# Two layer norms finished in place during the following stage, value tiles cleared one projection later

## The chip, the cores and the metric

The kernel runs on one core of a Trainium2 chip. The metric is the device time of one execution in microseconds (us); the time before is the median of three executions. Names of engines: PE (TensorE, matrix products and transposes), DVE (VectorE), ACT (ScalarE), POOL (GpSimd), SP (SyncE, here only an issuer of DMAs). ACT issues DMAs too, on a queue of its own, in order with its computations.

## The reference

Two transformer blocks over 256 tokens of width 1024, in float32. The change lies in the first of them:

```
def _layer_norm(x, g, b):
    mu = jnp.mean(xf, axis=-1, keepdims=True)
    var = jnp.mean(jnp.square(xf - mu), axis=-1, keepdims=True)
    return ((xf - mu) * lax.rsqrt(var + LN_EPS)).astype(x.dtype) * g + b

for i in range(DEPTH):                       # DEPTH = 2
    h = swa(x) if i % 2 == 0 else nsa(x)     # window attention / sparse attention
    x = _layer_norm(DN_ALPHA * x + h, ln_gain[i, 0], ln_bias[i, 0])
    f = swiglu(x) if i % 2 == 0 else moe(x)  # 3584 hidden / 8 experts, 2 a token
    x = _layer_norm(DN_ALPHA * x + f, ln_gain[i, 1], ln_bias[i, 1])
```

So there are four layer norms, counted 0 to 3. Number 0 stands between the window attention and the SwiGLU, number 1 between the SwiGLU and the sparse attention. Each result is used twice: as the input of the next matrix products, and, untransposed, as the x of the next residual sum. The second block (a mixer, a cross-attention to 256 memory tokens, a feed-forward layer) follows; its memory tokens depend on nothing before them.

## The kernel before

The 256 tokens are two tiles of 128 rows, tt = 0 and 1 (in the orders and rows a tile name such as X or y stands for both, unless a number tells them apart). The stages are built one after the other: `swa`, `ffn0`, `nsa`, `moe`, then the second block. A float32 product is three matmuls: high part by high part, high by low, low by high. Weights come from HBM through SP's queue into nine raw tiles of 512 KB (`w`); ACT copies out the high half (`wh`, lines 253 and 256), DVE subtracts to get the low half (`wl`, lines 254 and 257), into a ring of five split tiles from which PE reads. A 512 KB tile of `ffn0` feeds 24 matmuls.

The instructions of each engine run in one fixed order that a scheduler works out when the kernel is built, from dependences, priorities and memory: a tile that finds no free on-chip memory waits in that order until a pool is closed. `issue_after(i)` adds that what follows may not be placed ahead of instruction i; it adds no wait on the chip.

A layer norm 0 or 1 goes as follows. `ln_part` makes the residual sum y and its statistics (lines 374, 375). `ln_norm` normalises y in place (line 397, two halves of 512 columns), PE transposes it (line 186), and `transpose_split` puts gain and bias on the transposed tile (lines 201 on DVE, 203 on ACT, tile `trg`) and splits it into `xh` (line 204, ACT) and `xl` (line 205, DVE), the input of the next products. `ln_end` then makes the untransposed result: gain and bias rows are broadcast to all partitions by two DMAs of 512 KB on ACT's queue (`gb`, `bb`), and X = y * gb + bb takes eight DVE operations of 128x512 (lines 441, 442).

Inside `ffn0`, after the second chunk of hidden columns, `memory_tokens` loads the memory tokens (tile `mem`, one buffer, twice 512 KB, line 1867), squares and scales them (lines 1872 to 1875) and has PE transpose them for a later product. At the start of `nsa`, small tables (`cm`, `vhalf`, `cval`, `pr`, `w2`) are loaded on ACT's queue, and the value tiles `vz` (lines 845, 846) and `kcc` are cleared behind the emission of the first projection (columns 1024 to 1535, which ends in the rotated tiles `two`, lines 823, 824). In the attention proper, with the pool `nsa3` open, PE fills waits with products of the memory tokens (line 1900).

`route_load` brings the router's weights `rt` and three tables (`first`, `slots`, `uf`) by DMA on ACT's queue and puts the gain of layer norm 2 on the weights (`gb` again, line 968; column sums, line 970). `moe` then makes the logits: PE multiplies by `gb` (line 1002), DVE adds the norm's parts (lines 1007, 1008, tile `L`), picks two experts a token (lines 1014 to 1022, `sel`, `selb`), PE counts places (lines 1025 to 1029), and a branch on the counts follows. Four tiles of 1 MB (`parked`) of the experts' weights are loaded at that time.

Of the kernel before, what the change touches and what calls it, by code (L numbers as in the profile page):

```python
# [8 lines left out]
F32 = mybir.dt.float32  # L9
# [3 lines left out]
OP = mybir.AluOpType  # L13
AX = mybir.AxisListType
PSUM = bass.MemoryType.PSUM

P = 128
D = 1024
# [6 lines left out]
def f(ap):  # L25
    return ap.bitcast(F32)
# [72 lines left out]
class Net:  # L99
# [287 lines left out]
    def ln_norm(self, tt):  # L387

        nc = self.nc
        idx = self.ln  # L390
        if idx == 2:
            return self.ln_rows(tt)
        mu, rs = self.ln_stats(tt)
        y = self.y[tt]
        for h in range(2):
            yh = y[:, h * 512:h * 512 + 512]
            nc.vector.tensor_scalar(yh, yh, mu, rs, op0=OP.subtract, op1=OP.mult)
        if not self.ln_xT:
            self.new_xT()
            self.ln_xT = True  # L400
        gc = self.cols[:, idx * 8:(idx + 1) * 8]
        bc = self.cols[:, 32 + idx * 8:32 + (idx + 1) * 8]
        self.transpose_split(y, KD, self.xh[:, :, tt * P:(tt + 1) * P], self.xl[:, :, tt * P:(tt + 1) * P], gc, bc)
# [23 lines left out]
            nc.scalar.copy(Xh[:, s], y[:, s])  # L427
            nc.vector.tensor_sub(self.Xl[:, tt, s], y[:, s], f(Xh[:, s]))

    def ln_end(self):  # L430

        nc, A = self.nc, self.A
        li, lj = divmod(self.ln, 2)
        with self.pool("lng", 1) as lp:
            gb = self.bcast(A["ln_gain"][li, lj], D, "gb", pool=lp)
            bb = self.bcast(A["ln_bias"][li, lj], D, "bb", pool=lp)
            for tt in range(2):
                x = self.xp.tile([P, D], F32, tag=f"X{tt}", name=f"X{tt}")
                for c in range(0, D, 512):
                    cs, e = slice(c, c + 512), (nc.vector, nc.vector)[tt]  # L440
                    e.tensor_mul(x[:, cs], self.y[tt][:, cs], gb[:, cs])
                    e.tensor_add(x[:, cs], x[:, cs], bb[:, cs])
                self.X[tt] = x


    def rope64(self, pool, src, tt, nh, pairs=False):
# [55 lines left out]
    def heads_out(self, oh, ol, W, idx):  # L502

        def view(w, r0, nk, c0, n):
            for half in range(2):
                r = r0 // 512 * 512 + r0 % 512 // 2 + half * 256
                src = W[r:r + nk * 64, c0:c0 + n]
                self.nc.sync.dma_start(w[half * 64:half * 64 + 64, :, :n], src.rearrange("(g d) n -> d g n", d=64))

        self.ln_begin(idx)  # L510
        self.gemm(lambda k, tt: (oh[:, k, tt * P:(tt + 1) * P], ol[:, k, tt * P:(tt + 1) * P]), W, KD,
                  [(0, 512), (512, 512)], self.ln_part, view=view, apart=(1,))
        self.fine = False
        if idx == 0:
            self.ln_end()

    def swa(self):
        nc, A, tc = self.nc, self.A, self.tc
# [95 lines left out]
    def ffn_body(self, Wg, g0, Wu, u0, dff, Wd, emit, scale=None, beside=lambda p: None):  # L614

        nc, tc = self.nc, self.tc
        nkf = dff // P
        chunks = [(j, min(512, dff - j)) for j in range(0, dff, 512)]
        with ExitStack() as c:
            p = c.enter_context(self.pool("ffn", 1))  # L620
# [11 lines left out]
            j, n = chunks[0]  # L632
# [20 lines left out]
            for j, n in chunks[1:]:  # L653
                s = p.tile([P, 4, T], F32, tag="silT", name="sil", bufs=2)
                k0 = j // P

                def gate(b, ps):
                    x = s[:, 2 * b:2 * b + 2]
                    if R is not None:
                        nc.vector.tensor_mul(x, ps, R.unsqueeze(1).to_broadcast([P, 2, T]))  # L660
                    nc.scalar.activation(x, x if R is not None else ps, AF.Silu)

                def up(b, ps):
                    x, k = s[:, 2 * b:2 * b + 2], k0 + 2 * b
                    nc.vector.tensor_mul(x, x, ps)
                    nc.scalar.copy(hh[:, k:k + 2], x)
                    nc.vector.tensor_sub(hl[:, k:k + 2], x, f(hh[:, k:k + 2]))

                self.gemm_f(Wg, g0 + j, n, gate)
                self.gemm_f(Wu, u0 + j, n, up)  # L670
                if j == 512:
                    beside(p)
# [22 lines left out]
    def ffn0(self):  # L695
        A = self.A
        self.ln_begin(1)
        self.mems = ExitStack()
        p = self.mems.enter_context(self.pool("memt", 1))
        self.mhl = [p.tile([P, 8, T], F32R, name=f"mem{n}") for n in "hl"]  # L700
        self.ffn_body(A["ffn_w_gate"][0], 0, A["ffn_w_up"][0], 0, 3584, A["ffn_w_down"][0], self.ln_part, beside=self.memory_tokens)
        self.ln_end()


    def nsa(self):
        nc, A, tc = self.nc, self.A, self.tc
        self.fine = True
        with ExitStack() as c0:
            po = c0.enter_context(self.pool("heads", 1))
            po.tile([P, 16], F32, name="lead")  # L710
            c = c0.enter_context(ExitStack())
            p = c.enter_context(self.pool("nsa", 1))
# [3 lines left out]
            zero = p.tile([P, 1], F32, name="zero")  # L716
            nc.vector.memset(zero, 0.0)
            vz = {b: [p.tile([P, 2, 4, P], F32R, name=f"v{b}{n}") for n in "hl"] for b in "sw"}
# [3 lines left out]
            kcc = [p.tile([P, 2, 2, 16], F32R, name=f"kc{n}") for n in "hl"]  # L722
            gate = [p.tile([P, 16, 3], F32, name=f"gate{tt}") for tt in range(2)]
            cm = p.tile([P, 2, 16], F32, name="cm")
            nc.scalar.dma_start(cm, A["cmask"].rearrange("t p c -> p t c"))
            cmb = p.tile([P, 2, 16], BF16, name="cmb")
            nc.vector.tensor_copy(cmb, cm)
            vhalf = p.tile([96, P], F32, name="vhalf")
            nc.scalar.dma_start(vhalf, A["vhalf"])
            cval = p.tile([P, 2], F32, name="cval")  # L730
            nc.scalar.dma_start(cval, A["cvalid"].rearrange("t p c -> p (t c)"))
            with ExitStack() as cc:
                self.turns = 1
                cp = cc.enter_context(self.pool("cmp", 1))
# [1 line left out]
                pos = cp.tile([P, 2, 16], F32, name="pos")  # L736
                for i, n in enumerate(("b_cmp_pos_k", "b_cmp_pos_v")):
                    pr = cp.tile([16, P], F32, tag="pr", name="pr")
                    nc.scalar.dma_start(pr, A[n][0].rearrange("(j l) d -> j (l d)", l=2))
                    tp = self.tr.tile([P, 512], F32, tag="tr", name="tr")  # L740
                    nc.tensor.transpose(tp[:, :16], pr, self.idn[:16, :16])
                    nc.vector.tensor_copy(pos[:, i], tp[:, :16])
                w2 = cp.tile([P, 2, 2, 2, 64], F32, name="w2")
                for i, n in enumerate(("b_cmp_k_w2", "b_cmp_v_w2")):
                    for h in range(2):
                        nc.scalar.dma_start(w2[:, i, :, h], A[n][0].rearrange("(k p) d -> p k d", p=P))


                def windows(which, two):
# [63 lines left out]
                def emit(i, c0, n, ps, tts=(0, 1)):  # L813
                    if c0 == 1024:
                        twos = self.twos = self.twos if tts[0] else [[], []]
                        two = self.two = self.two if tts[0] else po.tile([P, 2, 2, 4, 2, 64], F32, tag="oh", name="two")
                        for tt in tts:
                            u, t = self.rope64(a2, ps[tt][:, :256].rearrange("p (h d) -> p h d", d=64), tt, 4)
                            for w in range(2):
                                twos[w].append(two[:, w, tt])  # L820
                            v = ps[tt][:, 256:512].rearrange("p (h d) -> p h d", d=64)
                            both = lambda x: x.unsqueeze(2).to_broadcast([P, 4, 2, 64])
                            nc.vector.tensor_add(twos[0][tt], both(u), both(t))
                            nc.scalar.copy(twos[1][tt], both(v))
                    for tt in tts:
                        if c0 == 1536:
                            self.k_heads(a2, ps[tt][:, :256], kT["s"], tt)
# [12 lines left out]

                W = A["b_w_in"][0]
                self.gemm(self.xs, W, KD, [(1024, 512)], emit, apart=(0,))
                for z in vz["s"] + vz["w"]:
                    z = z.rearrange("p s v d -> p (s v d)")
                    nc.vector.tensor_copy(z[:, :512], zero.to_broadcast([P, 512]))
                    nc.scalar.copy(z[:, 512:], zero.to_broadcast([P, 512]))
                for k in kcc:
                    nc.gpsimd.tensor_copy(k.rearrange("p c h j -> p (c h j)"), zero.to_broadcast([P, 64]))
                self.gemm(self.xs, W, KD, [(1536, 512)], emit)
                win = windows(0, self.twos[0])  # L850
                self.gemm(self.xs, W, KD, [(2048, 256)], emit)
# [38 lines left out]
            for cc in range(2):  # L890
                for tt in range(2):
# [4 lines left out]
                    for half in range(2):  # L896
# [6 lines left out]
                        for b in range(4 // nh):  # L903
# [6 lines left out]
                                                     start=i == 0 and n == 0, stop=False)  # L910
                            nc.tensor.matmul(own, self.idb, self.maskb[:, 1:2].to_broadcast([P, 2 * nh, P]), start=False, stop=True)
                            gs = slice(b * nh, b * nh + nh)
                            nc.vector.tensor_reduce(nm[:, gs], sc.rearrange("p i r s j -> p i r (s j)"), axis=AX.X, op=OP.max, negate=True)
                            for i in range(nh):
                                g = b * nh + i
                                for r in range(2):
# [7 lines left out]
                        for r, br in enumerate("sw"):  # L924
                            for st in range(nst):
# [9 lines left out]
                                nc.tensor.matmul(ops, vl, ph, start=False, stop=False)  # L935
                                nc.tensor.matmul(ops, vh, pl, start=False, stop=False)
                        self.fill(1 / 16, SOON)
                    tp = self.tr.tile([96, 4, P], F32, tag="tr", name="tr")
                    for g in range(4):
                        nc.tensor.transpose(tp[:, g], f(pc[tt][:, cc * 4 + g]).rearrange("p n j -> p (n j)"), self.idn)  # L940
# [919 lines left out]
    def memory_tokens(self, p):  # L1860

        nc, A = self.nc, self.A
        h, l = self.mhl
        gc = self.cols[:, self.col["mem_kv_norm_2"]:self.col["mem_kv_norm_2"] + 8]
        for tt in range(2):
# [283 lines left out]
```

## Time and profile before

| | |
|---|---|
| median of 3 executions | 2332.0 us (2325.09 to 2341.94) |
| the profiled execution | 2328.03 us, span of the trace 2326.2 us |
| PE busy | 2229.0 us, 96% of the span |
| DVE busy | 1799.7 us, 77% |
| ACT busy | 1477.1 us, 63% |
| mean granted TensorE clock | 0.980 of full speed |

The stages by the trace, in us from the start of the span: window attention to about 100, SwiGLU to 342, projections of the sparse attention to about 436, attention and output product to 578, routing to 596, experts to about 1570, second block to the end. "Granted clock" is the share of the full TensorE clock that the chip allowed in a stretch; it is 1.0 or 0.5.

### The profile page before, as it was taken

What the parts mean: (1) busy time and instruction counts of PE and PEld (TensorE: products, weight loads), DVE (VectorE), ACT (ScalarE), POOL (GpSimd) and SP (SyncE); (2) the same over time, 40 slices, a digit from 0 to 9 for tenths busy, and PEclk for the clock granted to TensorE, in tenths of its full rate; (3) what the DMA queues carried; (4) which work ended last, traced back from release to release, by engine and by line L of the source; (5) the groups of instructions that cost most, each with busy time, mean ns of one, the idle gap of its engine ahead of it and who ended that gap; (6) DMA issues with size and microseconds to landing.
All of it is one profiled execution on the core that took longest, in us unless ns stands there. A gap on an engine that the chain in (4) does not pass through costs nothing.

```text
span 2326.2 us, 35748 instructions
## 1 busy us (share of the span) xinstructions
PE 2229.0 (96%) x12969; PEld 1930.2 (83%) x12969; DVE 1799.7 (77%) x2854; ACT 1477.1 (63%) x2390; POOL 66.8 (3%) x78
## 2 busy tenths in 40 slices
PE   8999998999899999999999999996999899999998
PEld 6699987878788888888888888885889888988997
DVE  7765558766899999999999999997866855666664
ACT  5654436575687778787878777874553554455553
POOL 0000000000000000000000000001110110000000
PEclk9999999999899999999999999998999999999999
DMA  8366655434999999999999999984323323544751
GB/s 246 96 203 190 192 167 172 156 103 142 318 372 369 342 354 370 366 373 329 364 373 369 341 358 370 368 300 117 109 73 101 94 62 107 162 154 165 229 195 46
DMA packets 319708, 541.92 MB, mean 233 GB/s; under 512 B 21839, under 2 KB 95015, under 8 KB 319271
## 3 DMA queue, kind: packets, MB, share of 16 engines
q1 hardware_dynamic: 309680, 528.93, 66.7%
q10 hardware_dynamic: 9847, 10.67, 1.5%
q8 instruction: 103, 1.69, 0.3%
q14 instruction: 78, 0.64, 0.1%
HBM read 536.38 MB, written 3.15 MB: 232 GB/s over the span
## 4 chain that ended last, share of the span: by engine, by line
PE 87%; DVE 6%; issue 3%; ACT 2%; DMA 1%; POOL 1%; SPq 0%; DVEq 0%; POOLq 0%; ACTq 0%
PE mm L1173 13%; PE mm L1175 13%; PE mm L1174 13%; PE mm L276 5%; PE mm L274 5%; PE mm L275 5%; PE mm L691 3%; PE mm L690 3%; PE mm L689 3%; PE mm L1900 2%; PE mm L318 1%; PE mm L319 1%; PE mm L317 1%; DVE wl L254 1%; PE sc L909 1%
## 5 line engine op out<-in xcount | busy, mean ns | idle before, releaser
L257 DVE TENSOR_TENSOR wl<-w,wh 128x1024 fp32r<-128x1024 f32 x755 | 905.9, 1222 | 182.3 <-ACT wh L256 155.1
L256 ACT CAST wh<-w 128x1024 fp32r<-128x1024 f32 x755 | 788.3, 1053 | 298.7 <-PE mm L1175 166.9
L1173 PE MATMUL mm<-wh,xg 128*128 128x512 f32 x896 | 354.1, 395 | 0.0
L1175 PE MATMUL mm<-wh,xg 128*128 128x512 f32 x896 | 349.6, 390 | 0.0
L1174 PE MATMUL mm<-wl,xg 128*128 128x512 f32 x896 | 349.2, 390 | 0.0
L253 ACT CAST wh<-w 128x512 fp32r<-128x512 f32 (+1 forms) x362 | 207.3, 615 | 125.4 <-PE mm L276 56.1
L254 DVE TENSOR_TENSOR wl<-w,wh 128x512 fp32r<-128x512 f32 (+1 forms) x362 | 237.1, 682 | 42.4 <-ACT wh L253 40.4
L1175 PEld LDWEIGHTS mm<-wh,xg 128*128 128x128 f32 x896 | 168.4, 188 | 35.9
L1174 PEld LDWEIGHTS mm<-wl,xg 128*128 128x128 f32 x896 | 168.6, 188 | 33.5
L1173 PEld LDWEIGHTS mm<-wh,xg 128*128 128x128 f32 x896 | 168.5, 188 | 33.4 <-DVE xg L1111 0.2
L689 PE MATMUL mm<-xh,wh 128*128 128x256 f32 x672 | 187.2, 279 | 0.0
L690 PE MATMUL mm<-xh,wl 128*128 128x256 f32 x672 | 187.1, 278 | 0.0
L691 PE MATMUL mm<-xl,wh 128*128 128x256 f32 x672 | 187.1, 278 | 0.0
L1174 PE MATMUL mm<-wl,h 128*128 128x512 f32 x448 | 175.2, 391 | 0.0
L1173 PE MATMUL mm<-wh,h 128*128 128x512 f32 x448 | 174.9, 390 | 0.0
L1175 PE MATMUL mm<-wh,h 128*128 128x512 f32 x448 | 174.5, 389 | 0.0
L689 PEld LDWEIGHTS mm<-xh,wh 128*128 128x128 f32 x672 | 127.4, 190 | 0.0
L690 PEld LDWEIGHTS mm<-xh,wl 128*128 128x128 f32 x672 | 126.1, 188 | 0.0
L691 PEld LDWEIGHTS mm<-xl,wh 128*128 128x128 f32 x672 | 126.2, 188 | 0.0
L248 DVE SCALAR_TENSOR_TENSOR wl<-w,cols,wh 128x512 fp32r<-128x512 f32 (+1 forms) x128 | 77.7, 649 | 47.2 <-ACT wh L247 47.1
L247 ACT ACTIVATE wh<-w,cols 128x512 fp32r<-128x512 f32 (+1 forms) x128 | 74.6, 635 | 45.1 <-issue 23.2
L1175 PEld LDWEIGHTS mm<-wh,h 128*128 128x128 f32 x448 | 84.1, 188 | 18.0 <-issue 0.5
(620 smaller groups left out, 4494.1 us busy)
## 6 DMA issues: line engine op xcount, KB each, us to landing
w<-in_moe_w_gate_dram SPq DMA_DIRECT2D x224, 512.0 KB, 5.5
w<-in_moe_w_up_dram SPq DMA_DIRECT2D x224, 512.0 KB, 5.6
w<-in_moe_w_down_dram SPq DMA_DIRECT2D x216, 512.0 KB, 5.8
w<-in_w_in_dram SPq DMA_DIRECT2D x60, 512.0 KB, 3.9
w<-in_w_ffn_in_dram SPq DMA_DIRECT2D x40, 512.0 KB, 9.8
w<-in_ffn_w_gate_dram SPq DMA_DIRECT2D x28, 512.0 KB, 4.4
w<-in_ffn_w_up_dram SPq DMA_DIRECT2D x28, 512.0 KB, 4.4
w<-in_ffn_w_down_dram SPq DMA_DIRECT2D x28, 512.0 KB, 3.6
```

Source lines behind the costliest of these rows:

```text
L253: nc.scalar.copy(wh[:, ks, :n], w[:, ks, :n])
L254: nc.vector.tensor_sub(wl[:, ks, :n], w[:, ks, :n], f(wh[:, ks, :n]))
L256: nc.scalar.copy(wh[:, :nk, :n], w[:, :nk, :n])
L257: nc.vector.tensor_sub(wl[:, :nk, :n], w[:, :nk, :n], f(wh[:, :nk, :n]))
L274: nc.tensor.matmul(o, h, wh[:, k, :sn], start=k0 + k == 0, stop=False)
L275: nc.tensor.matmul(o, h, wl[:, k, :sn], start=False, stop=False)
L689: nc.tensor.matmul(o, wh[:, k, js], h, start=first and j % 2 == 0, stop=False)
L690: nc.tensor.matmul(o, wl[:, k, js], h, start=False, stop=False)
L691: nc.tensor.matmul(o, wh[:, k, js], l, start=False, stop=last and j % 2 == 1)
L1173: nc.tensor.matmul(ps, h, wh[:, k], start=k0 + k == 0, stop=False)
L1174: nc.tensor.matmul(ps, h, wl[:, k], start=False, stop=False)
L1175: nc.tensor.matmul(ps, l, wh[:, k], start=False, stop=k0 + k == nk - 1)
```

## The change

`ln_norm` writes the normalised rows into the tile X instead of back into y. `ln_end` becomes a function that puts gain and bias on X in place, from one broadcast tile named `mem` at a time: gain first, then, in the same buffer, bias. For layer norm 0 it is called at the head of `memory_tokens` and shares that function's single `mem` buffer; for layer norm 1 it is called in the attention, in halves of 512 columns, with a `mem` buffer in the pool `nsa3`. The small tables of `nsa` go to SP's queue. The clears are placed behind the last two `two` operations, and `kcc` is cleared by DVE.

```diff
@@ ln_norm
-        y = self.y[tt]
+        y = self.X[tt] = self.xp.tile([P, D], F32, tag=f"X{tt}", name=f"X{tt}")
...
-            nc.vector.tensor_scalar(yh, yh, mu, rs, op0=OP.subtract, op1=OP.mult)
+            nc.vector.tensor_scalar(y[:, cs], self.y[tt][:, cs], mu, rs, op0=OP.subtract, op1=OP.mult)
@@ ln_end
+    def ln_end(self, pool, ins, width=D):
...
+        with self.tc.issue_after(ins):
+            for n, op in (("ln_gain", OP.mult), ("ln_bias", OP.add)):
+                for c in range(0, D, width):
+                    w = self.bcast(A[n][li, lj, c:c + width], width, "mem", pool=pool)
+                    for a in range(0, width, 512):
+                        for tt in range(2):
+                            x = self.X[tt][:, c + a:c + a + 512]
+                            nc.vector.tensor_tensor(x, x, w[:, a:a + 512], op=op)
@@ ffn_body, up
-                    nc.vector.tensor_mul(x, x, ps)
+                    self.last = nc.vector.tensor_mul(x, x, ps)
@@ nsa (and the same for vhalf, cval, pr, w2)
-            nc.scalar.dma_start(cm, A["cmask"].rearrange("t p c -> p t c"))
+            nc.sync.dma_start(cm, A["cmask"].rearrange("t p c -> p t c"))
@@ nsa, behind the first projection
-                for z in vz["s"] + vz["w"]:
...
-                    nc.gpsimd.tensor_copy(k.rearrange("p c h j -> p (c h j)"), zero.to_broadcast([P, 64]))
+                with tc.issue_after(self.last[0].ins), tc.issue_after(self.last[1].ins):
+                    for z in vz["s"] + vz["w"]:
...
+                        nc.vector.tensor_copy(k.rearrange("p c h j -> p (c h j)"), zero.to_broadcast([P, 64]))
@@ nsa, attention
+                        if cc == 0 and tt == 0 and half == 1:
+                            self.ln_end(ap, last.ins, 512)
@@ memory_tokens
+        self.ln_end(p, self.last.ins)
```

Lines of the changed kernel are two or three lower than before from line 430 on (441 is now the operation in place, 961 the load of `rt`, 999 the logits).

What the scheduler makes of it, at three places. First, DVE between the SwiGLU and the sparse attention, around the norm of the second token tile. Before (X with the number 3528 is tile 0, 3533 tile 1):

```order
L382 BN_AGGR mv<-st_1160 128x2
L441 TENSOR_TENSOR X_3528<-y_1157,gb 128x512
L349 TENSOR_SCALAR rs<-mv 128x1
L441 TENSOR_TENSOR X_3528<-y_1157,gb 128x512
L397 TENSOR_SCALAR y_1158<-y_1158,mv,rs 128x512 x2
L442 TENSOR_TENSOR X_3528<-X_3528,bb 128x512 x2
L201 TENSOR_SCALAR trg<-tr,cols 128x128 x2
L441 TENSOR_TENSOR X_3533<-y_1158,gb 128x512
L201 TENSOR_SCALAR trg<-tr,cols 128x128 x2
```

The same place in the changed kernel:

```order
L254 TENSOR_TENSOR wl<-w,wh 128x512
L382 BN_AGGR mv<-st_1144 128x2
L254 TENSOR_TENSOR wl<-w,wh 128x512
L349 TENSOR_SCALAR rs<-mv 128x1
L254 TENSOR_TENSOR wl<-w,wh 128x512
L397 TENSOR_SCALAR X_3491<-y_1142,mv,rs 128x512 x2
L457 TENSOR_TENSOR ropet<-mm,rope 128x256
L458 TENSOR_TENSOR ropeu<-mm,rope 128x256
L201 TENSOR_SCALAR trg<-tr,cols 128x128 x2
L818 TENSOR_TENSOR two<-ropeu,ropet 128x512
L201 TENSOR_SCALAR trg<-tr,cols 128x128 x2
```

The X operations are gone from there, and splits of weights and the rotation of the first tile's projection stand in their places.

Second, DVE in `ffn0` at the end of the second chunk of hidden columns. Before, ahead of the second memory tile's scaling (`meml` is the low part of the first memory tile, transposed):

```order
L665 TENSOR_TENSOR sil<-sil,mm 128x512 x2
L257 TENSOR_TENSOR wl<-w,wh 128x1024
L667 TENSOR_TENSOR hl<-sil,hh 128x512 x2
L195 SCALAR_TENSOR_TENSOR meml<-tr,cols,memh 128x128 x3
L257 TENSOR_TENSOR wl<-w,wh 128x1024
```

In the changed kernel, from just behind the chunk's products (line 661, before 665) and the first two gain operations to the first memory tile's scaling (line 1873, before 1875); 1053 is X of tile 0, 1113 of tile 1:

```order
L663 TENSOR_TENSOR hl<-sil,hh 128x512 x2
L441 TENSOR_TENSOR X_1053<-X_1053,mem 128x512
L441 TENSOR_TENSOR X_1113<-X_1113,mem 128x512
L257 TENSOR_TENSOR wl<-w,wh 128x1024 x3
L441 TENSOR_TENSOR X_1053<-X_1053,mem 128x512
L441 TENSOR_TENSOR X_1113<-X_1113,mem 128x512
L441 TENSOR_TENSOR X_1053<-X_1053,mem 128x512
L441 TENSOR_TENSOR X_1113<-X_1113,mem 128x512
L257 TENSOR_TENSOR wl<-w,wh 128x1024 x3
L1871 TENSOR_TENSOR ss<-s_1601 128x1
L349 TENSOR_SCALAR ss<-ss 128x1
L1873 TENSOR_SCALAR mem<-mem,ss 128x1024
```

Four gain operations now precede three splits, four bias operations follow them, and the first memory tile is scaled only after three more splits. On PE its transposes stand 151 matmuls later than before (behind 391 instead of 240 matmuls of 256 columns), those of the second tile 82 matmuls behind the first's (85 before).

Third, ACT around the router's tables. Before, in the early projections of `nsa`:

```order
L824 COPY two<-mm 128x512
L253 CAST wh<-w 128x2x256
L964 DMA rt<-in_moe_router_dram 128x8x8
L253 CAST wh<-w 128x2x256
L976 DMA first<-in_first_dram 128x64
L978 DMA slots<-in_slots_dram 128x128
L981 DMA uf<-in_before_dram 128x128
```

In the changed kernel, at the end of layer norm 2, just ahead of the choice of experts:

```order
L427 CAST Xh<-y_5800 128x512 x2
L1123 ACTIVATE y_5800<-y_5800 128x512 x2
L961 DMA rt<-in_moe_router_dram 128x8x8
L973 DMA first<-in_first_dram 128x64
L975 DMA slots<-in_slots_dram 128x128
L978 DMA uf<-in_before_dram 128x128
L1039 ACTIVATE gate<-gate 128x16
```

These four loads have moved from the first projections to the end of the stage. What is made from them has moved with them: on DVE `gb`, `sums` and `ub` now stand between `Xl` and `L`, and on PE the product with `sums` and all sixteen logit matmuls follow the last transposes of y.

## Rows read from the trace of the kernel before

**Rows 1.** The page: busy time of the engines, and the chain that ended last.

```profile
PE 2229.0 (96%) x12969; PEld 1930.2 (83%) x12969; DVE 1799.7 (77%) x2854; ACT 1477.1 (63%) x2390; POOL 66.8 (3%) x78
PE 87%; DVE 6%; issue 3%; ACT 2%; DMA 1%; POOL 1%; SPq 0%; DVEq 0%; POOLq 0%; ACTq 0%
```

**Rows 2.** Stretches of the span, from:to, length; busy us (and instructions) of PE, PEld, DVE, ACT, POOL; granted clock; DMA share; GB/s.

```profile
118.00:121.40 3.40, 3.40 (x9) 2.63 (x8) 3.30 (x5) 1.84 (x2) 0.00 (x0) 0.50 0.12 19
...
356.90:363.80 6.90, 5.41 (x12) 3.41 (x13) 5.21 (x13) 5.72 (x12) 0.00 (x0) 0.51 0.26 61
...
460.00:575.00 115.00, 114.91 (x689) 92.09 (x688) 74.78 (x148) 74.63 (x209) 1.01 (x1) 1.00 0.38 113
...
582.00:596.00 14.00, 5.74 (x29) 5.38 (x30) 9.72 (x37) 5.17 (x8) 0.99 (x1) 0.51 0.75 253
```

**Rows 3.** PE at the first transition: start, us, operation, idle before it and releaser.

```profile
112.89 1.11 PE L186 MATMUL tr<-idn,y 128*128 128x128 f32 x8 [0.18 <-DVE y L397]
...
116.76 0.50 PE L274 MATMUL mm<-wh,xh 128*128 128x512 f32 x1 [2.52 <-ACT xh L204]
```

**Rows 4.** DVE at this transition, 99 to 122 us, by line: busy us, mean ns.

```profile
L441 DVE TENSOR_TENSOR X<-y,gb 128x512 f32<-128x512 f32 x4 | 2.6, 684 | 0.0
L257 DVE TENSOR_TENSOR wl<-w,wh 128x1024 fp32r<-128x1024 f32 x2 | 2.4, 1221 | 0.1
```

**Rows 5.** PE at the second transition.

```profile
354.56 1.12 PE L186 MATMUL tr<-idn,y 128*128 128x128 f32 x8 [0.56 <-DVE y L397]
...
357.78 0.28 PE L741 MATMUL tr<-idn,pr 16*128 16x16 f32 x1 [2.10 <-DVE trg L201]
```

**Rows 6.** All engines around the loading of the second memory tile, in order of time.

```profile
156.37 1.05 ACT L256 CAST wh<-w 128x1024 fp32r<-128x1024 f32 x1 [1.67 <-PE mm L691]
...
158.60 1.28 DVE L665 TENSOR_TENSOR sil<-sil,mm 128x512 f32<-128x512 f32 x2
...
159.09 1.05 ACT L256 CAST wh<-w 128x1024 fp32r<-128x1024 f32 x1 [1.67 <-PE mm L691]
...
159.96 0.35 SPq L1867 DMA_DIRECT2D mem<-in_mem_dram  x1
...
167.22 0.60 ACT L1872 ACTIVATE sq<-mem 128x512 f32<-128x512 f32 x1
...
169.74 0.75 DVE L1875 TENSOR_SCALAR mem<-mem,ss 128x1024 f32<-128x1024 f32 x1 [0.37 <-POOL ss L350]
...
170.64 1.06 PE L186 MATMUL tr<-idn,mem 128*128 128x128 f32 x8 [1.06 <-DVE mem L1875]
```

**Rows 7.** DMA issues from 345 to 600 us: count, KB, us to landing.

```profile
parked<-in_moe_w_down_dram SPq DMA_DIRECT2D x4, 1024.0 KB, 6.5
...
kv<-mkv SPq DMA_DIRECT2D x8, 256.0 KB, 2.7
...
gb<-in_ln_gain_dram ACTq DMA_DIRECT2D x1, 512.0 KB, 3.6
...
lnb<-in_ln_bias_dram ACTq DMA_DIRECT2D x1, 512.0 KB, 5.5
...
rt<-in_moe_router_dram ACTq DMA_DIRECT2D x1, 32.0 KB, 2.4
```

**Rows 8.** The router's work: all engines at 374 us and from 578 to 589 us.

```profile
374.75 0.35 DVE L968 TENSOR_TENSOR gb<-rt,cols 128x64 f32<-128x64 f32 x2
...
578.47 1.85 PE L1002 MATMUL at<-gb,xT 128*128 128x8 f32 x16
...
585.51 1.29 ACT L1126 ACTIVATE y<-y 128x512 f32<-128x512 f32 x2
...
586.05 0.21 DVE L1007 SCALAR_TENSOR_TENSOR L<-c,nm,at 128x8 f32<-128x8 f32 x1
...
588.46 0.17 DVE L1021 TENSOR_SCALAR selb<-sel 128x16 bf16<-128x16 f32 x1
...
588.68 0.17 PE L1025 MATMUL at<-selb,ub 128*128 128x8 bf16 x1 [5.95 <-DVE selb L1021]
```

More of the change, by code (lines that the diff above doesn't have):

```diff
@@ L389, in ln_norm @@
         nc = self.nc
-        idx = self.ln
+        idx = self.ln_X = self.ln
         if idx == 2:
@@ L393, in ln_norm @@
         mu, rs = self.ln_stats(tt)
-        y = self.y[tt]
+        y = self.X[tt] = self.xp.tile([P, D], F32, tag=f"X{tt}", name=f"X{tt}")
         for h in range(2):
-            yh = y[:, h * 512:h * 512 + 512]
-            nc.vector.tensor_scalar(yh, yh, mu, rs, op0=OP.subtract, op1=OP.mult)
+            cs = slice(h * 512, h * 512 + 512)
+            nc.vector.tensor_scalar(y[:, cs], self.y[tt][:, cs], mu, rs, op0=OP.subtract, op1=OP.mult)
         if not self.ln_xT:
@@ L428, in ln_rows @@
             nc.vector.tensor_sub(self.Xl[:, tt, s], y[:, s], f(Xh[:, s]))
-    def ln_end(self):
+    def ln_end(self, pool, ins, width=D):
         nc, A = self.nc, self.A
[L433 to L443, printed above, removed]
+        li, lj = divmod(self.ln_X, 2)
+        with self.tc.issue_after(ins):
[6 more added lines that the diff above has]
+                            nc.vector.tensor_tensor(x, x, w[:, a:a + 512], op=op)
     def rope64(self, pool, src, tt, nh, pairs=False):
@@ L513, in heads_out @@
         self.fine = False
-        if idx == 0:
-            self.ln_end()
     def swa(self):
@@ L701, in ffn0 @@
         self.ffn_body(A["ffn_w_gate"][0], 0, A["ffn_w_up"][0], 0, 3584, A["ffn_w_down"][0], self.ln_part, beside=self.memory_tokens)
-        self.ln_end()
     def nsa(self):
@@ L728, in nsa @@
             vhalf = p.tile([96, P], F32, name="vhalf")
-            nc.scalar.dma_start(vhalf, A["vhalf"])
+            nc.sync.dma_start(vhalf, A["vhalf"])
             cval = p.tile([P, 2], F32, name="cval")
-            nc.scalar.dma_start(cval, A["cvalid"].rearrange("t p c -> p (t c)"))
+            nc.sync.dma_start(cval, A["cvalid"].rearrange("t p c -> p (t c)"))
             with ExitStack() as cc:
@@ L738, in nsa @@
                     pr = cp.tile([16, P], F32, tag="pr", name="pr")
-                    nc.scalar.dma_start(pr, A[n][0].rearrange("(j l) d -> j (l d)", l=2))
+                    nc.sync.dma_start(pr, A[n][0].rearrange("(j l) d -> j (l d)", l=2))
                     tp = self.tr.tile([P, 512], F32, tag="tr", name="tr")
@@ L745, in nsa @@
                     for h in range(2):
-                        nc.scalar.dma_start(w2[:, i, :, h], A[n][0].rearrange("(k p) d -> p k d", p=P))
+                        nc.sync.dma_start(w2[:, i, :, h], A[n][0].rearrange("(k p) d -> p k d", p=P))
                 def windows(which, two):
@@ L822, in emit @@
                             both = lambda x: x.unsqueeze(2).to_broadcast([P, 4, 2, 64])
-                            nc.vector.tensor_add(twos[0][tt], both(u), both(t))
-                            nc.scalar.copy(twos[1][tt], both(v))
+                            self.last = (nc.vector.tensor_add(twos[0][tt], both(u), both(t)), nc.scalar.copy(twos[1][tt], both(v)))
                     for tt in tts:
@@ L842, in nsa @@
                 self.gemm(self.xs, W, KD, [(1024, 512)], emit, apart=(0,))
-                for z in vz["s"] + vz["w"]:
[L844 to L847, printed above, removed]
-                    nc.gpsimd.tensor_copy(k.rearrange("p c h j -> p (c h j)"), zero.to_broadcast([P, 64]))
+                with tc.issue_after(self.last[0].ins), tc.issue_after(self.last[1].ins):
+                    for z in vz["s"] + vz["w"]:
+                        z = z.rearrange("p s v d -> p (s v d)")
+                        nc.vector.tensor_copy(z[:, :512], zero.to_broadcast([P, 512]))
+                        nc.scalar.copy(z[:, 512:], zero.to_broadcast([P, 512]))
+                    for k in kcc:
+                        nc.vector.tensor_copy(k.rearrange("p c h j -> p (c h j)"), zero.to_broadcast([P, 64]))
                 self.gemm(self.xs, W, KD, [(1536, 512)], emit)
@@ L912, in nsa @@
                             gs = slice(b * nh, b * nh + nh)
-                            nc.vector.tensor_reduce(nm[:, gs], sc.rearrange("p i r s j -> p i r (s j)"), axis=AX.X, op=OP.max, negate=True)
+                            last = nc.vector.tensor_reduce(nm[:, gs], sc.rearrange("p i r s j -> p i r (s j)"), axis=AX.X, op=OP.max, negate=True)
                             for i in range(nh):
```

## Prediction, from the kernel before

> **What bounds the kernel now.** I read the page first: PE is busy 96% of the span and makes up 87% of the chain that ended last, DVE 6% of it, though DVE is busy 77% of the time [rows 1]. So DVE work removed anywhere is worth nothing in itself; the change can win only where PE waits for DVE, and lose where it makes PE wait. The waits of PE, looked up stage by stage, then told where that is. At the two transitions whose norms are changed PE stands still for 2.52 us [rows 3] and for 2.10 us [rows 5], each behind the chain normalise, transpose, `trg`, split, and works at half the full clock afterwards [rows 2]. In the SwiGLU it waits once, 1.06 us, for the second memory tile [rows 6]. In the attention it does not wait: 114.91 of 115 us busy [rows 2]. In the routing it waits 5.95 us for `selb` [rows 8], and of 14 us there it is busy 5.74, at a clock of 0.51 [rows 2]. The experts, 950 us, are PE at its pace; nothing lost ahead of them comes back there. The sum is made against the profiled execution, 2328.0 us, which lies 4.0 below the median of 2332.0.
>
> **First transition (window attention to SwiGLU).** Eight DVE operations of 0.68 us leave it [rows 4], 5.4 us, but only part of that stands on PE's path. Between the second tile's normalisation and PE's return at 116.76 two of them stand ahead of the first `trg` and one between the `trg` pairs. They cost at most 3 x 0.68 = 2.0 us there, by estimate half of it, since DVE would have waited for the transposes anyway. Against this the scheduler puts a whole split of 1.22 us [rows 4] ahead of the norm of the second tile, which by estimate delays it by 0.8 of these 1.22; in return six more matmuls run before the transposes instead of after. The bound above is all of the idle time, 2.52 + 0.18 [rows 3], with the clock: 3.4 us at half speed [rows 2] do 1.7 us of work, so 4.4. The bound below is nothing. I take -1.3, nearer the small end, because the chain norm, transposes, `trg`, split itself stays whole, and it alone is longer than what PE has left to do.
>
> **Second transition (SwiGLU to sparse attention).** The same eight operations go. On DVE three splits take the places ahead of the norm, and the rotation (`ropet`, `ropeu`, `two`) those between the `trg` pairs, as the order shows. PE's waits of 0.56 and 2.10 us [rows 5] and the half-clock stretch of 6.9 us [rows 2] are what can be had; a shorter wait takes at most part of the clock's loss. I take -1.2, with 0 and -2.8 as ends. The tables moved to SP are five small loads ahead of which PE has weights in the ring; `cmb`, now early on DVE, waits for one of them, at a moment when DVE has time. The clears, four of DVE and four of ACT, get behind 48 matmuls of the next projection: nothing.
>
> **Memory tokens.** Here a wait is added. The `mem` buffer serves gain, bias and two memory tiles in turn. The chain, in times of the trace of before: the chunk's products at 158.60 [rows 6] end at 159.9; four gain operations of 0.68 [rows 4] with the two `hl` between them, until about 163.7. ACT then issues the bias broadcast, which needs 3.6 to 5.5 us to land as `gb` and `lnb` did, 512 KB each [rows 7]: 167.3 to 169.2. Four bias operations: 170.0 to 171.9. SP, which waits for them, loads the memory tile (512 KB, at least the 3.6 of `gb`): about 174 to 176. Squares on ACT, with splits between them, the scale's root and the scaling on DVE: 167.22 to 170.49 for the second tile before [rows 6], 3.3 us, with two splits in between rather 4 to 5. So the tile is ready between 178 and 181. PE reaches its transposes 151 matmuls, 6.3 weight tiles, later than before; a tile lasts 2.72 us (ACT's casts at 156.37 and 159.09, each released by PE [rows 6]), so at 158.6 + 17.1 = 175.7. PE waits 2.3 to 5.3 us, 4.2 in my estimate. After waits like that of rows 3 the clock was at 0.5 for 3.4 us [rows 2], which would be another 1.7. The second tile has the same chain as before and 82 matmuls of cover instead of 85, so its 1.06 us stay. Queued behind the waiting issues are weight loads on SP and casts on ACT; the rings of nine and five tiles (five are 13.6 us of PE) cover those. Together +5.5, ends +2 and +8.
>
> **Attention.** Eight operations of 0.68 us and four broadcasts of 256 KB come in. DVE has 40 us to spare in the 115 [rows 2], so 5.4 us of work fit. But each broadcast shares one buffer with the last, so it is issued only when DVE is done with the one before, and DVE, which works in order, stands until it lands: 2.7 us for 256 KB of `kv` [rows 7]. The softmax waits behind that; PE has memory products to fill with. I take +1.5; ends -3 (the order of PE's work there is new as well) and +6.
>
> **Routing.** This is the largest term, and a side effect: the router's four loads now stand behind ACT's last work on y. Before, `rt` and what DVE makes of it were done at 375 [rows 8], and the logits ran under the norm. Now: ACT ends at 585.51 + 1.29 = 586.8 [rows 8]; `rt` lands after 2.4 us as at 369 us, or up to the 6.5 of a `parked` load, in whose company it is [rows 7]; I take 4. `gb`: 0.35. The logits, 32 passes: twice 1.85 us [rows 8] at full clock, up to 6.4 if the passes last nearly twice as long at the half clock of this stretch [rows 2]; I take 4.9. From the first `L` to `selb` it was 588.46 - 586.05 = 2.4. That gives `selb` at 598.5 instead of 588.46: +10, with ends of +7.2 (2.4 and 3.7) and +14. Nothing covers it, since PE has no other work before the branch.
>
> The weights stream with three quarters of the DMA engines' time in that stretch [rows 2], and `lnb`, beside such a stream, took 5.5 us where `gb` took 3.6 [rows 7]; so a load is longer in company. The Trainium skill, "DMA: Bandwidth & Descriptors", section "Queues, rings and completion order", says that each DMA engine goes round its queues in turn, a packet at a time. By that the 32 KB of `rt` would not stand behind the megabytes of SP's queue but pass between them, close to the 2.4 us; the term would be 8.4 and the whole 1.6 less. No run here shows a load this small beside the `parked` ones.
>
> **Sum.** -1.3 - 1.2 + 5.5 + 1.5 + 10 = +14.5: 2342.5 by the profiled execution, 2346.5 by the median. I say 2345.
>
> **Rivals.** (a) The transitions give nothing: splits and rotation merely take the X operations' places. For it speaks that PE's waits are for the last link of a chain, not for a busy DVE; against it, that the X operations stand inside that chain. +2.5 on the sum: about 2347. (b) The change does only what it says, and the new waits are hidden. The transitions win all, -4.4 - 2.8, the memory tile comes in time, and the tables land while DVE still works on y: -7.2, so 2321 by the profiled execution and 2325 by the median. Against it speaks the order of ACT, in which the loads stand behind y. (c) The broadcasts in the attention stop PE. One mechanism: DVE in order, standing at an operation whose operand is not there, with the softmax behind it. The price is 4 x (2.7 to 5.5 us of landing), 11 to 22 us, and some half clock after each; with 16 in place of 1.5 the time is about 2360, over 1% slower. It decides once PE's filler lasts shorter than a landing; 0.09 us of idle time in 115 [rows 2] says that the filler has been long enough so far.
>
> **How the numbers follow.** Chances: the forecast 0.62, (a) 0.16, (b) 0.07, (c) 0.15. A measurement of this kernel tells about 1%, 23 us, from no change. The forecast's ends are -4.4 - 2.8 + 2 - 3 + 7.2 = -1 and 8 + 6 + 14 = +28 if all fall on one side; with half of that either way and the scatter of the three times, 2328 to 2360, which takes in (a) and half of (c). Faster by over 1% (under 2309) needs more than (b) gives: 0.02. Slower by over 1% (over 2355): (c) and the upper edge of the forecast, 0.18. The rest, 0.80, within 1%.
>
> **What would show it.** In the changed trace: idle time of PE at its first transposes of `mem` in the SwiGLU of 2 to 5 us; `selb` some 10 us later behind y than before, with `rt` landing after 587; PE idle at the two transitions about 1 us shorter each; no new wait of PE in the attention over 1 us. I am wrong if `rt` is landed when DVE has finished `Xl`, if PE waits for DVE during the attention, or if the half-clock stretches at the transitions vanish.

## The result, and the profile after

The changed kernel takes 2353.5 us (median of 20, 2337.4 to 2364.1) against 2336.0 us (median of 20, 2325.1 to 2344.5). The ratio is 1.0066 with a 95% interval of 1.0049 to 1.0084: about 15 us slower, under 1%. The forecast was 2345 us, range 2328 to 2360, made of a sum of +14.5 us on the profiled execution. Executions of one kernel scatter by some 20 to 27 us, so what follows rests on ratios, and, within a trace, on intervals of one stage.

The profiled execution's span is 2345.8 us against 2326.2, 19.6 us more. Where PE waits in the changed kernel, three questions to the view of waits (engine, line, operation, releaser: us, times, longest), for the SwiGLU's first chunks (145 to 195 us), the second transition (335 to 372) and the routing (575 to 620):

```profile
PE tr L186 <- DVE mem L1873: 3.8, 2, 3.3
```

```profile
PE tr L736 <- DVE trg L201: 1.9, 1, 1.9
PE tr L186 <- DVE X L397: 0.9, 2, 0.5
PE mm L274 <- ACT xh L204: 0.4, 1, 0.4
```

```profile
PE at L970 <- DVE sums L967: 14.8, 1, 14.8
PE mm L1103 <- DVE cnt L1130: 2.3, 1, 2.3
PE at L1022 <- DVE selb L1018: 2.3, 1, 2.3
PE tr L417 <- ACT xT L418: 1.1, 1, 1.1
```

One wait stands out: 14.8 us for the column sums of the router's weights, work whose first step, `gb`, was done at 375 us in the kernel before [rows 8], some 220 us earlier. There PE waited only the 5.95 us for `selb` at this place [rows 8]. All engines there, in order of time:

```profile
585.11 1.15 SPq L220 DMA_DIRECT2D parked<-in_moe_w_down_dram  x2
...
587.08 0.68 DVE L428 TENSOR_TENSOR Xl<-y,Xh 128x512 fp32r<-128x512 f32 x1
587.14 1.29 ACT L1123 ACTIVATE y<-y 128x512 f32<-128x512 f32 x2
587.81 0.39 ACTq L961 DMA_DIRECT2D rt<-in_moe_router_dram  x1
...
595.94 0.36 DVE L965 TENSOR_TENSOR gb<-rt,cols 128x64 f32<-128x64 f32 x2 [7.96 <-DMA rt<-in_moe_router_dram]
...
597.22 6.97 PE L999 MATMUL at<-gb,xT 128*128 128x8 f32 x32
...
604.23 0.22 DVE L1004 SCALAR_TENSOR_TENSOR L<-c,nm,at 128x8 f32<-128x8 f32 x1 [2.79 <-PE at L999]
606.25 0.17 DVE L1018 TENSOR_SCALAR selb<-sel 128x16 bf16<-128x16 f32 x1
```

The load is issued at 587.81, and DVE can use it at 595.94, 8.1 us later, on the heels of two `parked` megabytes. Then the logits take 7.0 us (597.22 to 604.19), at a granted clock of 0.50. From the last `Xl` to `selb` it is 606.25 - 587.08 = 19.2 us. Before, that last `Xl` began at 585.46, as the same view of the kernel before shows:

```profile
585.46 0.68 DVE L428 TENSOR_TENSOR Xl<-y,Xh 128x512 fp32r<-128x512 f32 x1
```

With `selb` at 588.46 [rows 8] that makes 3.0 us. So the routing costs 16.2 us more, most of the result. The stretches that answer to [rows 2] (columns as there):

```profile
116.00:122.00 6.00, 5.80 (x25) 4.80 (x26) 3.71 (x4) 3.68 (x5) 0.00 (x0) 1.00 0.06 9
...
170.00:180.00 10.00, 6.69 (x47) 6.49 (x46) 4.90 (x10) 5.08 (x12) 0.55 (x1) 0.83 0.51 162
460.00:575.00 115.00, 114.87 (x695) 92.76 (x694) 79.23 (x158) 75.43 (x213) 1.51 (x2) 1.00 0.41 119
582.00:612.00 30.00, 10.65 (x53) 10.52 (x54) 12.11 (x46) 5.72 (x10) 0.99 (x1) 0.56 0.57 180
```

The half clock is gone from the first transition in this execution, and a new dip stands at 170 to 180, behind the wait for the first memory tile. In the attention PE is as full as before; DVE has 4.4 us more to do there (79.23 against 74.78) and PE does not wait for it. The chain that led to that wait:

```profile
155.30 1.28 DVE L661 TENSOR_TENSOR sil<-sil,mm 128x512 f32<-128x512 f32 x2
156.50 1.28 DVE L441 TENSOR_TENSOR X<-X,mem 128x512 f32<-128x512 f32 x2
...
158.90 1.29 DVE L441 TENSOR_TENSOR X<-X,mem 128x512 f32<-128x512 f32 x2
...
160.22 0.33 ACTq L172 DMA_DIRECT2D mem<-in_ln_bias_dram  x1
```

```profile
163.96 2.50 DVE L441 TENSOR_TENSOR X<-X,mem 128x512 f32<-128x512 f32 x4 [0.36 <-DMA mem<-in_ln_bias_dram]
...
166.48 0.35 SPq L1865 DMA_DIRECT2D mem<-in_mem_dram  x1
```

```profile
171.53 0.60 ACT L1870 ACTIVATE sq<-mem 128x512 f32<-128x512 f32 x1 [3.32 <-DMA mem<-in_mem_dram]
...
175.37 0.75 DVE L1873 TENSOR_SCALAR mem<-mem,ss 128x1024 f32<-128x1024 f32 x1 [0.67 <-POOL ss L350]
...
176.18 1.11 PE L186 MATMUL tr<-idn,mem 128*128 128x128 f32 x4 [3.31 <-DVE mem L1873]
```

Gain, bias and memory tile pass through one buffer: the bias is issued the moment the last gain operation is done (160.2), lands 3.7 us later, is added until 166.5, the memory tile is issued then, is usable 5.0 us later, and is scaled at 175.4.

### The profile page after: what moved, and what is told of

Its sections match the earlier page's. It is cut to its first block, busy times and chain, and to the rows that moved or that the text cites. A ratio compares the mean times of both kernels' runs of the same rounds, so it can differ in the third digit from the quotient of the medians.

```text
span 2345.8 us, 35756 instructions
## 1 busy us (share of the span) xinstructions
PE 2235.3 (95%) x12969; PEld 1940.4 (83%) x12969; DVE 1801.6 (77%) x2856; ACT 1478.4 (63%) x2390; POOL 66.2 (3%) x76
## 4 chain that ended last, share of the span: by engine, by line
PE 65%; DVE 4%; issue 3%; ACT 1%; POOL 1%; DMA 0%; DVEq 0%; POOLq 0%; ACTq 0%
PE mm L1170 13%; PE mm L1172 13%; PE mm L1171 13%; PE mm L276 2%; PE mm L275 2%; PE mm L274 2%; PE mm L686 1%; PE mm L687 1%; PE mm L685 1%; PE mm L318 1%; PE mm L319 1%; PE mm L317 1%; PE tr L1202 1%; PE tr L1773 1%; PE at L1784 1%
```

## The experiments

Each run has a short name, e1 to e10. The theory after the result: the router's tables are late because the attention's pool has grown by the `mem` buffer, and that alone is worth about 16 us; the shared `mem` buffer in the SwiGLU is worth a few more. The rival: the broadcasts and DVE operations put into the attention are the loss, and the tables only show it elsewhere. All edits are to the changed kernel unless said otherwise.

**The changed kernel again (e1).** 

> The changed kernel once more, beside its variants. Ratio to the kernel before 1.005 to 1.008. In its trace the router's weights land 6 to 10 us after their issue and PE waits 12 to 16 us for the column sums. Open is the FFN's rhythm: in the first trace its matmuls of 256 columns came 3 to 4% further apart behind the wait for the memory tile. If that hangs on the order of PE's instructions, it is there again; if it is an accident of one execution, it may be missing.

Ratio 1.007 (1.0042 to 1.0097). PE waited 15.4 us for the column sums, 3.6 us for the first memory tile. The half clock at the first transition was back in this execution (0.83 over 115 to 125 us, as before; 1.00 in the first trace of the changed kernel). The slower rhythm of the FFN's matmuls was there again.

**Tables early (e2).**

```diff
-    def ln_end(self, pool, ins, width=D):
+    def ln_end(self, pool, ins, width=D, tag="mem"):
...
-                    w = self.bcast(A[n][li, lj, c:c + width], width, "mem", pool=pool)
+                    w = self.bcast(A[n][li, lj, c:c + width], width, tag, pool=pool)
...
-                            self.ln_end(ap, last.ins, 512)
+                            self.ln_end(ap, last.ins, 512, "mkv")
```

> The second norm's gain and bias go through the buffer mkv of the memory products, so that the pool of the attention needs no more room than before; the router's loads then stand in the first projections again. Theory (the late tables are most of the loss): 16 us faster than the changed kernel, ratio to before 0.998 to 1.002, no wait of PE for the column sums, selb about 3 us behind the last Xl. Rival (the loss is the broadcasts and the additional DVE work in the attention, the tables only shift it): ratio stays at 1.005 to 1.007.

Ratio 0.9998 (0.9975 to 1.002). The loads are back in the first projections, `selb` comes 3.0 us after the last `Xl`, and the waits of PE from 575 to 620 us are those of before:

```profile
PE at L1022 <- DVE selb L1018: 6.2, 1, 6.2
PE mm L1103 <- DVE cnt L1130: 2.3, 1, 2.3
```

The eight in-place operations and the four broadcasts are still in the attention, some 20 us later and sharing a tile with the memory products; only the room that their own buffer took is gone. The rival falls: it expected 1.005 or more. The ratio lies some 17 us below that of the changed kernel on the same chip, about as much as the routing had lost in the trace.

**Memory tokens unchained (e3).** Gain and bias of layer norm 0 go to the two y tiles of the next norm, which are idle then.

```diff
-                    w = self.bcast(A[n][li, lj, c:c + width], width, "mem", pool=pool)
+                    if pool is None:
+                        w = self.y[n == "ln_bias"]
+                        nc.scalar.dma_start(w, A[n][li, lj].partition_broadcast(P))
+                    else:
+                        w = self.bcast(A[n][li, lj, c:c + width], width, "mem", pool=pool)
...
-        self.ln_end(p, self.last.ins)
+        self.ln_end(None, self.last.ins)
```

> Gain and bias of the first norm are loaded into the two y tiles of the next norm, idle at that time, instead of the memory tokens' buffer; nothing else. Theory (the shared buffer chains four loads): PE's wait of 3.3 us for the first memory tile goes, 4 to 5 us faster than the changed kernel, ratio 1.003 to 1.005; if the slower rhythm of the FFN's matmuls came from that wait or from the place of the transposes, another 3 us, 1.002 to 1.003. Rival (the wait was covered by something else that is late next): ratio 1.006 to 1.008.

Ratio 1.0052 (1.0026 to 1.0077), against 1.007 of the changed kernel on the same chip: some 4 us, but the two intervals overlap, and 1.0052 lies just outside the ranges of both theory and rival. The time alone does not show the gain. In the trace the wait is gone: from 145 to 195 us PE waits once, as before [rows 6]:

```profile
PE tr L186 <- DVE mem L1877: 1.0, 1, 1.0
```

**Both (e4).** The two edits together (the attention's buffer is `mkv`, the SwiGLU's are the y tiles).

> Both of these. Theory: the gains add up, 20 to 24 us faster than the changed kernel, ratio to before 0.996 to 0.999, with the gains of the two transitions (about 4 us together) and of the attention (about 1.6 us) left over. Rival (the losses hide one another, or the gains at the transitions are accidents): ratio 0.999 to 1.003.

Ratio 0.9989 (0.9971 to 1.0008). Both new waits are gone in its trace. The ratio stands at the edge of the theory's range, where the rival's begins, and its interval takes in 1, so the distance from the kernel before was not settled by this.

**Without the parked loads (e5).**

```diff
-            last = [self.xp.tile([P, 4, 512], F32, tag="xh", name="parked"), *(p.tile([P, 4, 512], F32, name=f"parked{n}") for n in range(3))]
-            for n, t in enumerate(last):
-                self.park(Wd[NE - 1], (NF - 16 + n * 4) * P, 512, t)
```

> The changed kernel without the four parked loads of 1 MB (the last expert's weights then come through the ring like all others). The router's tables stay late in ACT's order. Theory (they are late to land because they wait in company with the parked megabytes): the router's weights land 2.5 to 4 us after their issue instead of 8, PE's wait for the column sums shrinks from 14.8 to 9 to 11 us, 4 to 6 us faster than the changed kernel, ratio to before 1.004 to 1.005 unless the last expert starves. Rival (a load of 32-byte pieces is slow by itself when late): landing stays at 7 us or more, ratio 1.006 to 1.008.

Ratio 1.0055 (1.0032 to 1.0078). The load at its late place, now without the parked megabytes (order of time, all engines):

```profile
589.87 0.39 ACTq L961 DMA_DIRECT2D rt<-in_moe_router_dram  x1
592.14 0.36 DVE L965 TENSOR_TENSOR gb<-rt,cols 128x64 f32<-128x64 f32 x2 [2.09 <-DMA rt<-in_moe_router_dram]
...
592.97 0.61 PE L970 MATMUL at<-sums,one 128*128 128x16 f32 x2 [8.92 <-DVE sums L967]
```

2.3 us instead of 8.1, near the 2.4 at its early place in the kernel before [rows 7], and PE's wait is 5.9 us shorter. The stretches from the load's issue to its use, in the kernel before, in this run and in the changed kernel, show how busy the DMA engines were meanwhile (the share is the last number but one):

```profile
368.90:371.30 2.40, 2.40 (x12) 1.95 (x11) 2.40 (x5) 1.55 (x3) 0.00 (x0) 1.00 0.59 123
```

```profile
589.87:592.10 2.23, 0.00 (x0) 0.00 (x0) 0.17 (x3) 0.62 (x1) 0.00 (x0) 0.50 0.56 115
```

```profile
587.80:595.90 8.10, 0.00 (x0) 0.00 (x0) 0.18 (x3) 0.63 (x1) 0.00 (x0) 0.50 0.98 321
```

So, by the traces, six of the sixteen microseconds are the company of the parked megabytes; ten are the late issue and the logits behind it. The whole kernel gained less, a ratio lower by 0.001 to 0.0015, with overlapping intervals and above the expected 1.004 to 1.005, so the times do not confirm the six.

**Tables on SP's queue (e6).** `nc.scalar.dma_start` becomes `nc.sync.dma_start` in all four loads of `route_load`.

> The changed kernel with the router's four loads on SP's queue, behind the first parked megabyte and ahead of two others, in time still behind the attention. Theory (company): the router's weights have about a third of the parked bytes ahead of them and land 3 to 6 us after their issue, PE's wait for the column sums falls to 9 to 12 us, ratio 1.004 to 1.006. Rival (only the place in the order of ACT counts, not the queue): the wait stays at 14 us or more, 1.006 to 1.008.

Ratio 1.0062 (1.0038 to 1.0087).

```profile
588.04 0.42 SPq L220 DMA_DIRECT2D parked<-in_moe_w_down_dram  x1
588.55 0.64 SPq L961 DMA_DIRECT2D rt<-in_moe_router_dram  x1
...
590.04 0.68 DVE L428 TENSOR_TENSOR Xl<-y,Xh 128x512 fp32r<-128x512 f32 x1
...
596.61 0.36 DVE L965 TENSOR_TENSOR gb<-rt,cols 128x64 f32<-128x64 f32 x2 [5.68 <-DMA rt<-in_moe_router_dram]
...
597.44 0.61 PE L970 MATMUL at<-sums,one 128*128 128x16 f32 x2 [12.50 <-DVE sums L967]
```

It lands 8.1 us after its issue here too, behind one parked megabyte instead of two and the weight tiles ahead of it: a miss of the expectation, which said 3 to 6. PE's wait is 2.3 us shorter than in the changed kernel, because the load is issued 1.5 us ahead of the last `Xl` and not 0.7 us behind it; at 12.5 us it lies between the ranges of theory and rival. Changing the queue did not shorten the landing; what the slow cases share are DMA engines busy 0.98 of the time.

**Tables of the attention and clears alone (e7).** The kernel before, with the last part of the change only (the DMAs of `cm`, `vhalf`, `cval`, `pr` and `w2` on SP, the clears behind `two`).

> The kernel before with one part of the change alone: the small tables of the sparse attention on SP's queue and the clears behind the first projection. Theory: no effect by itself, ratio 0.999 to 1.001, since PE waits at that transition for the chain of the norm. Rival (this part is the gain that the version with both mends keeps): 0.996 to 0.998.

Ratio 1.001 (0.9985 to 1.0036): no effect that the interval shows, and the rival, 0.998 or less, falls. In its trace PE waits 2.5 us for `trg` at the second transition, not less than before [rows 5].

**A slow memory load, twice (e8, e9).** The version with both mends; the tokens' columns arrive in another order, so that the results are other ones, and only the traces, one of each, are used.

```diff
-            nc.sync.dma_start(x, A["mem_2"][0, tt * P:(tt + 1) * P, :])
+            for a in range(2):
+                nc.sync.dma_start(x[:, a * 512:a * 512 + 512], A["mem_2"][0, tt * P:(tt + 1) * P, :].rearrange("p (b a c) -> p a b c", a=2, c=32)[:, a])
```

> The version with both mends, with the memory tokens loaded in pieces of 128 bytes and with blocks of columns in another order (the loaded values are permuted), so that the load is slow and PE waits for the second memory tile, while the order of all instructions is the same. For the FFN's rhythm: if a long wait with a drop of the clock inside the run of 256-column matmuls leaves the slower rhythm behind, the matmuls come every 117 to 118 ns after the wait instead of 113.3; if it is the place of the transposes in PE's order, they stay at 113.3.

> As the run before with pieces of 32 bytes instead of 128 (loaded values permuted again), since with 128 bytes the second memory tile came no later and PE waited only 1.0 us, which told nothing. Now a wait of over 3 us is expected at the second tile. If a long wait inside the run of 256-column matmuls leaves the slower rhythm, they come every 117 to 118 ns behind it; if not, 113.3.

 (`c=8` in place of `c=32`)

Both missed their aim: PE waited 1.0 and 1.4 us for the second tile, since the load, although it took up to 12.0 us in pieces of 32 bytes, ran under other work. The rhythm stayed at the quick one in both, which says nothing on a long wait.

**Both, again (e10).** 

> The version with both mends once more, for its distance from the kernel before: theory (the transitions' gains of 2 to 4 us are real and remain) 0.998 to 0.9995; rival (they are given back) 0.9995 to 1.002. In its trace selb stands 3 us behind the last Xl and PE's waits at the memory tiles are at most 1.1 us, as in its first trace.

Ratio 0.997 (0.9948 to 0.9992), with the first measurement 0.9989: by these two the version with both mends is 0.1 to 0.3% faster than the kernel before, though only the second interval lies below 1, and about 0.8 to 1% faster than the changed one. The rival falls; the theory's range ended at 0.998, so the gain came out larger than it said. As expected, `selb` stands 3.0 us behind the last `Xl` and PE's wait at the memory tiles is 1.1 us.

## Why the prediction was right, point by point

**First transition, -1.3.** PE's waits from 95 to 125 us fell from 4.2 us (2.5, 1.0 and 0.7 in the view of waits) to 3.3 (2.1 and 1.2), so -0.9. In the first trace the half-clock stretch vanished as well, for which the bound of -4.4 had left room; in the second trace of the same kernel it was there, and in e2, e5 and e6 too. A vanished half-clock stretch was named as a sign of being wrong; it appeared in one of five traces with this order, so here the clock's part is chance from one execution to the next, and the term was about right. None of the five traces with unchained memory tiles (e3, e4, e8, e9, e10) has the stretch; why is open.

**Second transition, -1.2.** The waits fell from 3.8 us (2.1, 1.1, 0.4 and 0.2) to 3.2 (1.9, 0.9 and 0.4 above). The clock over 356 to 372 us rose from 0.79 to 0.89 in the traces, which is 1.6 us of work; e7, with the norms as before, has 0.89 there too, so this part need not come from the change. Together that is in the range of 0 to -2.8. The splits and the rotation did take the places of the X operations, so rival (a) was right in its picture, though not in its price of nothing.

**Memory tokens, +5.5.** The wait of 3.3 us (2.3 to 5.3 forecast, 4.2 taken), 1.7 us by the clock that fell behind it (0.83 over 10 us is 3.4 us at half), and a wait for the second tile of 0.5 instead of 1.06: +4.4. The chain ran as written, counted from the end of the chunk's products, which came 3.3 us earlier than before (155.30 against 158.60); only its last load took 5.0 us instead of about 4. The term's own parts, 4.2 and 1.7, add up to 5.9 and not to 5.5.

**Attention, +1.5.** No new wait of PE, as the view of waits shows for the attention, and the term did not appear: from the first product with the compressed keys to the last `Xl` the changed kernel is 1.6 us shorter (below). Rival (c) falls, and with it the picture that this term shares with it. DVE hardly stood for a broadcast; its only wait for one from 436 to 578 us is

```profile
DVE X L441 <- DMA mem<-in_ln_gain_dram: 0.2, 1, 0.2
```

The eight operations stand from 459 to 480 us between others, and when DVE reached one, its operand was there.

**Routing, +10, ends +7.2 and +14.** The mechanism was right, and this is the term that was mis-sized: it measured +16.2. Two of its parts were too small. The landing of `rt` took 8.1 us where the range ended at 6.5, the time of one parked load; experiment e5 shows that without the parked loads it is 2.3. The logits took 7.0 us where it ended at 6.4. The prediction's ground for a longer load, `lnb` against `gb`, was thin: the DMA engines were busy 0.79 of the time beside the one and 0.68 beside the other, and `lnb` was issued 0.4 us behind another 512 KB on its own queue. What shows the company's part is e5. The sentence on the Trainium skill ("DMA: Bandwidth & Descriptors", "Queues, rings and completion order": each DMA engine goes round its queues in turn) was read as 2.4 us for the load; the measurement decides against that reading: the load could be used at 595.94, about when the second parked megabyte, 10.1 us after its own issue, had landed too.

**The sum against the trace.** The same work in both traces, first the kernel before, then the changed one: the last transposes of the second norm (354.56 in [rows 5]) and the first product with the compressed keys.

```profile
434.12 0.26 PE L872 MATMUL at<-kch,qh 128*128 128x32 f32 x1
```

```profile
359.79 1.11 PE L186 MATMUL tr<-idn,X 128*128 128x128 f32 x8 [0.42 <-DVE X L397]
...
437.35 0.26 PE L867 MATMUL at<-kch,qh 128*128 128x32 f32 x1
```

With the last `Xl` and `selb` above, the changed kernel is 5.2 us behind at the end of the SwiGLU, 3.2 at the compressed keys, 1.6 at the last `Xl`, 17.8 at `selb` and 19.6 at the end. Stage by stage that is +5.2 where the sum had +4.2 (first transition and memory tokens), -2.0 where it had -1.2, -1.6 where it had +1.5, +16.2 where it had +10, and +1.8 behind the routing, where it had nothing and no experiment looked. In the +5.2 are 3 to 4 us that the sum did not have: the matmuls of 256 columns went more slowly from about 185 to 280 us, and whether the change causes that is open (last section). So the routing came out 6.2 us too small and the attention 3.1 too large, and that the sum of +14.5 stands so near the 15 us of the ratio is in part luck; this pair of traces has 19.6.

**Where the hoped-for gain went.** At the two transitions PE waits 1.5 us less, and with the clock in the traces they give some 2 to 5 us. The version with both mends is faster than the kernel before by about that much (2.6 and 7 us by its two ratios). That its gain is that of the transitions is argued and not shown: e7 excludes the tables and the clears, but no run has the transitions alone. The changed kernel pays 16 us in the routing, through a buffer and not through the moved arithmetic, as e2 shows, and 4 in the memory tokens, as the waits in e3 show and the times do not contradict.

## What to carry to other kernels

A buffer added to a pool can move loads that have nothing to do with it: after such an edit, look where the loads of the following stages stand in each engine's order, not only at the lines that were edited. A tile that serves several loads in turn makes one chain of them, and an idle tile of the same shape is often at hand. A small table needed soon should be issued before the DMA engines are full: with the engines busy 0.59 of the time it landed in 2.4 us, and at 0.98, beside parked megabytes, it took 8.1. That a mechanism is possible, here DVE standing for a broadcast, does not say that it happens: the order shows how much other work stands between the load and its use.

## Unexpected

The matmuls of 256 columns in the SwiGLU have two rhythms at the same granted clock of 1.00. Stretches of 20 us (220 to 240 us, columns as in [rows 2]) of the kernel before, and, in the second fence, of the changed kernel:

```profile
220.00:240.00 20.00, 20.00 (x179) 20.00 (x178) 11.12 (x12) 9.80 (x12) 0.00 (x0) 1.00 0.69 192
```

```profile
220.00:240.00 20.00, 20.00 (x172) 20.00 (x172) 10.99 (x12) 9.01 (x10) 0.00 (x0) 1.00 0.65 184
```

179 matmuls against 172, 4% fewer. All five traces with the chained memory tiles (the changed kernel twice, e2, e5, e6) show 172 or 173; the traces of the kernel before and of the versions with unchained tiles (e3, e4, e8, e9, e10) show 179. That looked like a trace left behind by the long wait or by the place of the transposes, but e7, which has the order of the kernel before in this stage and waits only 1.1 us, shows 172 too, and needs 3.9 us more than the kernel before from its second memory tile's transposes to the first product with the down weights (169.66 to 273.62 against 170.64 to 270.73). So neither is needed for it, and what sets the rhythm stays open.
